# Summing five modulation vectors over the partitions with a GpSimd library instruction and an accumulating DMA instead of TensorE

## The chip, the cores and the metric

One core of a Trainium2 chip runs the whole kernel. The metric is the device time in microseconds (us) of one execution. The engines are named as in the profile: PE is TensorE (matmul), DVE is VectorE, ACT is ScalarE, POOL is GpSimd, and SP is SyncE, which here only issues DMAs.

## The reference

Two layers run over 256 latent tokens (x) and 256 context tokens (ctx) of width 1024. Each layer is a half-step SwiGLU, a token mixer (layer 0: neighbourhood attention, layer 1: a short gated convolution), and another half-step SwiGLU. Each sub-layer is modulated by vectors that come from a conditioning vector `c` through one large matrix `ada_w`:

```python
s_c = jax.nn.silu(c)
for i in range(DEPTH):                                   # DEPTH = 2
    m = (s_c @ ada_w[i] + ada_b[i]).reshape(B, N_MOD, 1, D)      # 9 vectors of 1024
    x = half_step_ffn(x, m[:, 0], m[:, 1], m[:, 2], ffn_w_in[i, 0], ffn_w_out[i, 0], ...)
    hx = modulate(x, m[:, 3], m[:, 4])                   # x * (1 + scale) + shift
    y_lat = attention or convolution of hx
    x = post_norm_update(x, y_lat, m[:, 5], 1.0, ...)    # LayerNorm(alpha*x + w*gate*y)
    x = half_step_ffn(x, m[:, 6], m[:, 7], m[:, 8], ffn_w_in[i, 1], ffn_w_out[i, 1], ...)
```

A vector is written (l, m): layer l, number m of nine. The change concerns the last five, (1,4) to (1,8).

## The kernel before

**The matmuls.** Every fp32 product of the layers is made of three fp32r matmuls: a weight block is loaded raw (`w1r`, `w2r`, by `wunit`), ACT copies its high part (`w1h`, line 210), DVE subtracts for the low part (`w1l`, line 213), and `mmu` (lines 164 to 167) multiplies high by high, high by low and low by high. PE's order is the program's own (a manual schedule); on DVE, ACT, POOL and SP a scheduler orders the instructions, and each engine then runs its list strictly in that order.

**A SwiGLU** (`ffn`) has 11 panels of `ffn_w_in`, each with four weight units and two token tiles, then a product with `ffn_w_out`. When a panel's PSUM bank is full, ACT makes `sil` (line 478) and DVE multiplies it with the other half of the bank (line 479). Four steps later PE transposes the two `sil` tiles (`gT`, line 487), ACT copies the result to `gh`, and DVE makes `gl` (line 113).

**The modulation vectors** are made in the background of these panels by `ada`. For one vector it loads eight 128 x 1024 blocks of `ada_w` (`ar`, line 303, on SP) and DVE accumulates each, times a per-partition scalar, into a tile `acc` of 128 x 1024 (lines 294 and 296, two halves of 512). When all vectors of a group are accumulated, and a few steps later, PE sums `acc` over the partitions by a matmul with ones (`ps`, tile name `ada`, line 327), DVE adds the bias row `adab` (line 328, tile `adar`), and SP writes the rows to `scr` in DRAM (line 330). From there `fold_cols` (tile `mrow`, line 360) and `mod_rows` (tile `gate`, line 345) read them back for the LayerNorm that uses them.

Behind attention there are three such groups: (1,4) and (1,5) during the second SwiGLU of layer 0, (1,6) and (1,7) during the first of layer 1, and (1,8) during the last. The pool `hp` is re-opened behind attention; `acc` has two buffers.

**POOL** does little there: two small instructions per LayerNorm tile (`rs`, lines 402 and 403), and a memset of `adab`.

Of the kernel before, what the change touches and what calls it, by code (L numbers as in the profile page):

```python
# [2 lines left out]

# [6 lines left out]
F32 = mybir.dt.float32  # L10
F32R = mybir.dt.float32r
AF = mybir.ActivationFunctionType
ALU = mybir.AluOpType
# [3 lines left out]
P = 128  # L17
D = 1024
FF = 2816
KC = D // P  # L20
# [50 lines left out]
def backbone_kernel(  # L71
# [6 lines left out]
    nc = tc.nc  # L78
    sync = nc.sync
# [8 lines left out]
    hp = phase.__enter__()  # L88
# [6 lines left out]
    def nm(s):  # L95
        uid[0] += 1
        return f"{s}_{uid[0]}"
# [10 lines left out]
    def tpb(s="tp"):  # L108
        return bank("tp", s)
# [125 lines left out]
    ones = cp.tile([P, 32], F32, tag="ones", name="ones")  # L235
    ident = cp.tile([P, P], F32, tag="ident", name="ident")
    make_identity(nc, ident)
    lnc = cp.tile([P, 2], F32, tag="lnc", name="lnc")
# [4 lines left out]
    warm = cp.tile([1, 1], F32, tag="warm", name="warm")  # L243
# [24 lines left out]
    scr = [tc.dram_tile([2, 9 * D], F32, name=f"scr{i}") for i in range(2)]  # L268
    xscr = tc.dram_tile([2 * P, D], F32, name="xscr")


    bias_rows = []
    gate_ins = []

    def ada(vecs):


        acc = {}

        def accumulate(l, m, k, w):  # L280
            with ExitStack() as st:
                for i in gate_ins:
                    st.enter_context(tc.issue_after(i.ins))
                for i, vec in enumerate(vecs):
                    if vec[:2] != (l, m):
                        continue
                    if k == 0:
                        a = hp.tile([P, D], F32, tag="acc", bufs=2, name=nm("acc"))
                        acc[i] = [a[:, 0:512], a[:, 512:D]]
                    sc = cst[:, k, vec[2]:vec[2] + 1]  # L290
                    for h in range(2):
                        src, a = w[:, h * 512:(h + 1) * 512], acc[i][h]
                        if k == 0:
                            nc.vector.tensor_scalar(a, src, sc, None, op0=ALU.mult)
                        else:
                            nc.vector.scalar_tensor_tensor(out=a, in0=src, scalar=sc, in1=a,  # L296
                                                           op0=ALU.mult, op1=ALU.add)

        loaded = []
        for l, m in dict.fromkeys((l, m) for l, m, _ in vecs):  # L300
            for k in range(KC):
                w = hp.tile([P, D], F32, tag="ar", bufs=3, name=nm("ar"))
                sync.dma_start(w, ada_w[l, k * P:(k + 1) * P, m * D:(m + 1) * D])
                loaded.append((l, m, k, w))
                if len(loaded) > (ADA_LAG if gate_ins else 0):
                    accumulate(*loaded.pop(0))
                yield 1
        while loaded:
            accumulate(*loaded.pop(0))
            if loaded:  # L310
                yield 1
        n = 2 * len(vecs)
        if not bias_rows:
            bias_rows.append(hp.tile([P, 512], F32, tag="adab", name=nm("adab")))
            nc.gpsimd.memset(bias_rows[0], 0.0)
        bt = bias_rows[0]
        for i, (l, m, v) in enumerate(vecs):
            sync.dma_start(bt[64 * i:64 * i + 64:32], ada_b[l, m * D:(m + 1) * D].rearrange("(a b) -> a b", b=512))
        yield 1
        yield 1  # L320
        yield 1
        rows = hp.tile([P, 512], F32, tag="adar", name=nm("adar"))
        ps = tpb("ada")
        for i in range(len(vecs)):
            for h in range(2):
                j = 2 * i + h
                nc.tensor.matmul(ps[32 * j:32 * j + 32, :], ones, acc[i][h], start=True, stop=True)  # L327
        nc.vector.tensor_tensor(out=rows[:32 * n], in0=ps[:32 * n], in1=bt[:32 * n], op=ALU.add)
        for i, (l, m, v) in enumerate(vecs):
            sync.dma_start(scr[l][v, m * D:(m + 1) * D].rearrange("(a b) -> a b", b=512),  # L330
                           rows[64 * i:64 * i + 64:32, :])
        yield 1
# [3 lines left out]
    def stream(*groups):  # L336
        for g in groups:
            yield from ada(g)
            made[0] += 1
            if made[0] == ADA_SLOW:  # L340
                background[1] = ADA_FAST
# [359 lines left out]
    for q, (k0, n) in enumerate(steps):  # L701
        nxt = start_step(*steps[q + 1]) if q < 4 else iter(())
        for g in range(6 * n):
            for _ in range(NS[min(q, 2)][g]):
                next(nxt, 0)
            k = k0 + g // 6
# [319 lines left out]
    hp = phase.__enter__()  # L1026
# [35 lines left out]
    for i in range(len(steps) + LAG + V_LAG):  # L1062
# [27 lines left out]
        j = i - LAG - V_LAG  # L1090
# [14 lines left out]
    hTs, later = box  # L1105
    phase = tc.tile_pool(name="ph2", bufs=1)
    hp = phase.__enter__()
    bias_rows.clear()
    ext[0] = 3

    set_background(stream([(1, 4, 0), (1, 5, 0)]), 0.35, HOLD)
# [16 lines left out]
    w = sc_w_in[0]  # L1128
# [103 lines left out]
```

## Time and profile before

| what | value |
| --- | --- |
| median of three runs | 1262.23 us (1261.55 to 1262.94) |
| span of the profiled execution | 1259.9 us |
| granted PE clock | 0.998 |
| busy: PE, DVE, ACT, POOL | 1245.4, 952.5, 589.9, 41.4 us |
| matmuls of line 327, all ten groups | 76 records, three groups (20 records) behind attention |

The profiled execution is known by its span, from the first to the last instruction; the profile gives no other time for it, and the median of the runs lies 2.3 us above that span. A row of the timeline has start, duration (of x instructions in a row), engine, line, operation, out<-in with shapes, and in brackets how long the engine idled before it and who released it. Matmul ends are modelled and successive matmuls overlap, so distances between starts tell what one costs. SPq is SP's queue, where only the issue of a DMA is seen.

### The profile page before, as it was taken

How to read it: one execution, taken by the hardware profiler on the slowest of the kernel's cores; microseconds unless marked ns; L12 is line 12 of the kernel's file. 1: busy time of each engine (PE TensorE's matmuls, PEld its weight loads, DVE VectorE, ACT ScalarE, POOL GpSimd, SP SyncE). 2: the span in 40 equal slices, each digit the busy share in tenths (PEclk: the TensorE clock that was granted, in tenths of full speed). 3: DMA queues.
4: the chain of work that ended last, by engine and by line, in shares of the span. 5: the costliest groups of instructions: out<-in, count | busy, mean ns of one | idle time of the engine just before them, and what ended most of it. 6: DMA issues, size and time to landing. Idle time of an engine off the chain costs nothing.

```text
span 1259.9 us, 17303 instructions
## 1 busy us (share of the span) xinstructions
PE 1245.4 (99%) x5922; PEld 1007.2 (80%) x5922; DVE 952.5 (76%) x1678; ACT 589.9 (47%) x1152; POOL 41.4 (3%) x71
## 2 busy tenths in 40 slices
PE   9999999999999999999999999999999999999997
PEld 6787778777878877877888788888788887888786
DVE  3699987888878877889898546988546788876546
ACT  2432132312326456687655435655435644655431
POOL 0000000000001011121000000000000000000000
PEclk9999999999999999999999999999999999999999
DMA  9976678878842744465899645898645764886641
GB/s 300 310 241 215 197 239 280 269 255 266 300 149 85 217 93 92 93 130 170 256 342 318 225 144 169 285 340 268 214 145 170 247 202 131 262 289 184 223 158 55
DMA packets 202776, 268.59 MB, mean 213 GB/s; under 512 B 30090, under 2 KB 149362, under 8 KB 202688
## 3 DMA queue, kind: packets, MB, share of 16 engines
q1 hardware_dynamic: 202652, 267.48, 67.3%
q8 instruction: 46, 0.75, 0.2%
q14 instruction: 42, 0.34, 0.1%
q10 hardware_dynamic: 36, 0.02, 0.0%
HBM read 265.27 MB, written 2.17 MB: 212 GB/s over the span
## 4 chain that ended last, share of the span: by engine, by line
PE 92%; DVE 3%; ACT 3%; issue 1%; DMA 0%; POOL 0%; DVEq 0%; SPq 0%; ACTq 0%; POOLq 0%
PE f L679 19%; PE w L164 17%; PE w L167 17%; PE w L165 17%; PE wkv L164 2%; PE wkv L165 2%; PE wkv L167 2%; PE wc L164 2%; PE wc L167 2%; PE wc L165 2%; PE gT L487 1%; PE ada L608 1%; PE ada L327 1%; PE S L971 1%; ACT pr L979 1%
## 5 line engine op out<-in xcount | busy, mean ns | idle before, releaser
L210 ACT ACTIVATE w1h<-w1r 128x512 fp32r<-128x512 f32 (+1 forms) x352 | 199.8, 620 | 180.4 <-DMA w1r<-in_ffn_w_in_dram 73.3
L213 DVE TENSOR_TENSOR w1l<-w1r,w1h 128x512 fp32r<-128x512 f32 (+1 forms) x352 | 222.9, 679 | 44.6 <-ACT w1h L210 43.3
L164 PE MATMUL w<-w1h,hTh 128*128 128x512 f32 x528 | 209.4, 397 | 0.9 <-ACT hTh L112 0.9
L165 PE MATMUL w<-w1l,hTh 128*128 128x512 f32 x528 | 206.0, 390 | 0.2 <-DVE w1l L213 0.2
L296 DVE SCALAR_TENSOR_TENSOR acc<-ar,cst,acc 128x512 f32<-128x512 f32 x266 | 186.0, 746 | 15.4 <-DMA ar<-in_ada_w_dram 15.4
L164 PE MATMUL w<-w2h,gh 128*128 128x512 f32 (+1 forms) x446 | 173.4, 389 | 0.0
L165 PE MATMUL w<-w2l,gh 128*128 128x512 f32 (+1 forms) x446 | 172.1, 386 | 0.0
L213 DVE TENSOR_TENSOR w2l<-w2r,w2h 128x512 fp32r<-128x512 f32 x176 | 114.3, 688 | 76.0 <-ACT w2h L210 75.2
L210 ACT ACTIVATE w2h<-w2r 128x512 fp32r<-128x512 f32 x176 | 101.6, 624 | 146.0 <-PE w L167 103.6
L167 PE MATMUL w<-w1h,hTl 128*128 128x512 f32 x528 | 163.2, 390 | 0.3 <-DVE hTl L113 0.2
L167 PE MATMUL w<-w2h,gl 128*128 128x512 f32 (+1 forms) x446 | 136.1, 386 | 0.0
L679 PE MATMUL f<-h0h,w1h 128*128 128x512 f32 x352 | 133.3, 394 | 0.4 <-DVE h0h L634 0.4
L679 PE MATMUL f<-h0l,w1h 128*128 128x512 f32 x352 | 133.2, 391 | 0.0
L679 PE MATMUL f<-h0h,w1l 128*128 128x512 f32 x352 | 132.7, 390 | 0.0
L164 PEld LDWEIGHTS w<-w1h,hTh 128*128 128x128 f32 x528 | 99.2, 188 | 23.8 <-ACT hTh L112 1.7
L167 PEld LDWEIGHTS w<-w1h,hTl 128*128 128x128 f32 x528 | 98.9, 188 | 22.4 <-DVE hTl L113 1.5
L165 PEld LDWEIGHTS w<-w1l,hTh 128*128 128x128 f32 x528 | 99.2, 188 | 20.2 <-DVE w1l L213 0.6
L164 PEld LDWEIGHTS w<-w2h,gh 128*128 128x128 f32 x446 | 83.8, 188 | 19.2 <-issue 1.7
L165 PEld LDWEIGHTS w<-w2l,gh 128*128 128x128 f32 x446 | 83.8, 188 | 16.6
L167 PEld LDWEIGHTS w<-w2h,gl 128*128 128x128 f32 x446 | 83.3, 188 | 17.1
L679 PEld LDWEIGHTS f<-h0h,w1h 128*128 128x128 f32 x352 | 65.9, 189 | 18.8 <-issue 4.2
L679 PEld LDWEIGHTS f<-h0l,w1h 128*128 128x128 f32 x352 | 65.6, 188 | 14.3 <-issue 0.6
(186 smaller groups left out, 1684.5 us busy)
## 6 DMA issues: line engine op xcount, KB each, us to landing
w1r<-in_ffn_w_in_dram SPq DMA_DIRECT2D x340, 256.0 KB
ar<-in_ada_w_dram SPq DMA_DIRECT2D x128, 512.0 KB
w2r<-in_ffn_w_out_dram SPq DMA_DIRECT2D x88, 512.0 KB
ar<-in_ada_w_dram SPq DMA_DIRECT2D x32, 256.0 KB
wkvr<-in_na_w_qkv_dram SPq DMA_DIRECT2D x32, 256.0 KB
wcr<-in_sc_w_in_dram SPq DMA_DIRECT2D x32, 256.0 KB
wqr<-in_na_w_qkv_dram SPq DMA_DIRECT2D x8, 512.0 KB
wor<-in_na_w_out_dram SPq DMA_DIRECT2D x8, 512.0 KB
```

Of the source, the lines that this page charges most:

```text
L164: nc.tensor.matmul(ps, lh, rh, start=first and i == 0, stop=False)
L165: nc.tensor.matmul(ps, lh, rl, start=False, stop=False)
L167: nc.tensor.matmul(ps, ll, rh, start=False, stop=last and i == n - 1)
L210: nc.scalar.activation(hi[:, a:a + m // W_HI], raw[:, a:a + m // W_HI], AF.Copy)
L213: nc.vector.tensor_tensor(out=lo[:, a:b], in0=raw[:, a:b], in1=hi[:, a:b].bitcast(F32), op=ALU.subtract)
L296: nc.vector.scalar_tensor_tensor(out=a, in0=src, scalar=sc, in1=a, op0=ALU.mult, op1=ALU.add)
L327: nc.tensor.matmul(ps[32 * j:32 * j + 32, :], ones, acc[i][h], start=True, stop=True)
L487: nc.tensor.transpose(ps[:, j * 256 + i * P:j * 256 + (i + 1) * P], g[:, j * P:(j + 1) * P], ident)
L608: nc.tensor.matmul(ps[o:o + 32, 0:m], cst[:, a * kt + i, :], w[:, i, j, :], start=(a == 0 and i < 2), stop=(a == last and i >= kt - 2))
L679: nc.tensor.matmul(ps, w, hT0[k][part == 1], start=(k == part == 0), stop=(k == KC - 1 and part == 1))
L971: nc.tensor.matmul(banks[i], (qh, qh, ql)[f][ps, qs], (kh, kl, kh)[f][ps, :], start=f == 0, stop=f == 2)
L979: nc.scalar.activation(pr, S, AF.Exp, bias=mx[:, 0:1], accum_out=mx[:, 1:2])
```

## The change

From the end of attention on (`on_pool`), a vector is no longer summed on PE. As soon as its last block is accumulated, `summed` gives its `acc` to a library instruction of POOL, `partition_all_reduce`, which writes the sum over the partitions to all 128 partitions of a tile `red` (one buffer), and POOL issues a DMA that adds the first partition of `red` to `scr` in DRAM. For this the bias `ada_b` of the five vectors is copied into `scr` beforehand, in one DMA on SP. Behind a group's last vector, POOL reads `red` once in a one-element add (`warm`).

```diff
+from concourse.bass_isa import ReduceOp
...
+    on_pool = [False]
...
-                        a = hp.tile([P, D], F32, tag="acc", bufs=2, name=nm("acc"))
-                        acc[i] = [a[:, 0:512], a[:, 512:D]]
+                        acc[i] = hp.tile([P, D], F32, tag="acc", bufs=2, name=nm("acc"))
...
+            if on_pool[0] and k == KC - 1:
+                for i, vec in enumerate(vecs):
+                    if vec[:2] == (l, m):
+                        summed(i)
+
+        def summed(i):
+            l, m, v = vecs[i]
+            red = hp.tile([P, D], F32, tag="red", name=nm("red"))
+            nc.gpsimd.partition_all_reduce(red, acc[i], P, ReduceOp.add)
+            nc.gpsimd.dma_start(scr[l][v:v + 1, m * D:(m + 1) * D], red[0:1], accum_op=ALU.add)
+            if i == len(vecs) - 1:
+                nc.gpsimd.tensor_tensor(out=warm, in0=red[0:1, 0:1], in1=lnc[0:1, 0:1], op=ALU.add)
...
+        if on_pool[0]:
+            yield 1
+            return
         n = 2 * len(vecs)
...
-                nc.tensor.matmul(ps[32 * j:32 * j + 32, :], ones, acc[i][h], start=True, stop=True)
+                nc.tensor.matmul(ps[32 * j:32 * j + 32, :], ones, acc[i][:, h * 512:(h + 1) * 512], start=True, stop=True)
...
-    bias_rows.clear()
+    on_pool[0] = True
+    sync.dma_start(scr[1][0, 4 * D:9 * D].rearrange("(a b) -> a b", a=16), ada_b[1, 4 * D:9 * D].rearrange("(a b) -> a b", a=16))
```

How the instructions stand now (the line numbers of the changed kernel are up to 16 higher). POOL's list behind attention, before: two `rs` instructions for each LayerNorm tile, and the memset of the bias rows.

```order
L402 TENSOR_TENSOR rs_5661<-mv_5659,lnc 128x1
L403 TENSOR_TENSOR rs_5661<-rs_5661,lnc 128x1
L315 MEMSET adab_6712 128x512
L402 TENSOR_TENSOR rs_5744<-mv_5742,lnc 128x1
L403 TENSOR_TENSOR rs_5744<-rs_5744,lnc 128x1
L402 TENSOR_TENSOR rs_7409<-mv_7407,lnc 128x1
L403 TENSOR_TENSOR rs_7409<-rs_7409,lnc 128x1
```

The same place of POOL's list now. A bare ISA row is a change of the instruction library; `red<-acc` is the library's sum, which waits for DVE's last accumulation.

```order
L418 TENSOR_TENSOR rs_5744<-mv_5742,lnc 128x1
L419 TENSOR_TENSOR rs_5744<-rs_5744,lnc 128x1
L307 ISA
L307 ISA red_6385<-acc_6101 128x1024
L308 DMA scr_117<-red_6385 16x1x64
L307 ISA red_6716<-acc_6433 128x1024
L308 DMA scr_117<-red_6716 16x1x64
L310 ISA
L310 TENSOR_TENSOR warm<-red_6716,lnc 1x1
L418 TENSOR_TENSOR rs_7404<-mv_7402,lnc 128x1
```

The first library change has nothing to wait for and follows attention's last `rs`; the sums, their DMAs, the change back and `warm` now stand ahead of the next LayerNorm's `rs`.

PE's list in the second SwiGLU of layer 0, before: four matmuls with `ones` between two weight units.

```order
L164 MATMUL w_1269_6765<-w1h_6803,hTh_5819 128x512
L165 MATMUL w_1269_6765<-w1l_6804,hTh_5819 128x512
L167 MATMUL w_1269_6765<-w1h_6803,hTl_5820 128x512 x2
L327 MATMUL ada_6824<-acc_6100,ones 32x512 x2
L327 MATMUL ada_6824<-acc_6429,ones 32x512 x2
L164 MATMUL w_1268_6758<-w1h_6833,hTh_5724 128x512
L165 MATMUL w_1268_6758<-w1l_6834,hTh_5724 128x512
```

PE's list there now.

```order
L165 MATMUL w_1270_6769<-w1h_6807,hTh_5820 128x512
L166 MATMUL w_1270_6769<-w1l_6808,hTh_5820 128x512
L168 MATMUL w_1270_6769<-w1h_6807,hTl_5821 128x512 x2
L165 MATMUL w_1269_6762<-w1h_6828,hTh_5724 128x512
L166 MATMUL w_1269_6762<-w1l_6829,hTh_5724 128x512
```

Only the matmuls with `ones` are gone, here and in the two later groups (ten in all); DVE's list has lost three `adar` rows and is otherwise the same, with the panels' `w1l`, `sil` and `gl` in the same places between the accumulations.

SP's list in the same SwiGLU, before, at the place to which a read of `scr` moves (`mrow` is the 8 x 128 read of (1,4) for a later LayerNorm; it stood 27 rows further on, behind ten loads of `w2r`).

```order
L205 DMA w1r_6722<-in_ffn_w_in_dram 128x2x256 x2
L205 DMA w1r_6749<-in_ffn_w_in_dram 128x2x256 x2
L205 DMA w1r_6772<-in_ffn_w_in_dram 128x2x256 x2
L205 DMA w1r_6802<-in_ffn_w_in_dram 128x2x256 x2
L303 DMA ar_6597<-in_ada_w_dram 128x1024
```

SP's list there now.

```order
L206 DMA w1r_6726<-in_ffn_w_in_dram 128x2x256 x2
L206 DMA w1r_6753<-in_ffn_w_in_dram 128x2x256 x2
L206 DMA w1r_6776<-in_ffn_w_in_dram 128x2x256 x2
L376 DMA mrow_8707<-scr_117 8x128
L206 DMA w1r_6806<-in_ffn_w_in_dram 128x2x256 x2
L316 DMA ar_6601<-in_ada_w_dram 128x1024
```

The read of (1,4) now stands among the weight loads and waits there for POOL's DMA. The reads of (1,6) and (1,7) move forward in the same way in the next SwiGLU: (1,6) to just ahead of two `ar` loads, (1,7) to behind the second load of `w2r`. The ten small SP DMAs of the old way (bias in, rows out) are gone, and the one copy of the bias stands early in the first SwiGLU of layer 0.

More of the change, by code (lines that the diff above doesn't have):

```diff
@@ L287, in accumulate @@
                     if k == 0:
-                        a = hp.tile([P, D], F32, tag="acc", bufs=2, name=nm("acc"))
-                        acc[i] = [a[:, 0:512], a[:, 512:D]]
+                        acc[i] = hp.tile([P, D], F32, tag="acc", bufs=2, name=nm("acc"))
                     sc = cst[:, k, vec[2]:vec[2] + 1]
                     for h in range(2):
-                        src, a = w[:, h * 512:(h + 1) * 512], acc[i][h]
+                        src, a = (c[:, h * 512:(h + 1) * 512] for c in (w, acc[i]))
                         if k == 0:
```

## The prediction

> **What bounds the kernel now.** The page's first part comes first, then the busy times of the stage that the change touches, then the timeline there.
>
> ```profile
> PE 1245.4 (99%) x5922; PEld 1007.2 (80%) x5922; DVE 952.5 (76%) x1678; ACT 589.9 (47%) x1152; POOL 41.4 (3%) x71
> ...
> 597.00:784.00 187.00, 187.00 (x857) 153.45 (x856) 135.85 (x231) 96.59 (x185) 1.63 (x3) 1.00 0.74 246
> ```
>
> The second row is the second SwiGLU of layer 0 (length; then PE, PE's weight loads, DVE, ACT and POOL busy). PE has no gap in 187 us, so what is taken from PE shortens the stage, and what makes PE wait lengthens it. DVE is busy for 73% and POOL is free.
>
> **What is removed.** Busy time of the `ada` matmuls in three windows of 20 us (PE, weight loads, DVE), and PE's timeline without and with them:
>
> ```profile
> 700.00:720.00 20.00, 1.06 (x8) 0.16 (x8) 0.68 (x1) 1.00 0.60 205
> 880.00:900.00 20.00, 1.06 (x8) 0.16 (x8) 0.68 (x1) 1.00 0.67 225
> 1170.00:1190.00 20.00, 1.05 (x4) 0.14 (x4) 0.68 (x1) 1.00 0.58 191
> ```
>
> ```profile
> 698.00 0.61 PE L167 MATMUL w<-w1h,hTl 128*128 128x512 f32 x2
> ...
> 698.68 0.39 PE L165 MATMUL w<-w1l,hTh 128*128 128x512 f32 x1
> ...
> 703.94 0.61 PE L167 MATMUL w<-w1h,hTl 128*128 128x512 f32 x2
> 704.48 1.06 PE L327 MATMUL ada<-acc,ones 128*32 128x512 f32 x8
> ...
> 705.81 0.39 PE L165 MATMUL w<-w1l,hTh 128*128 128x512 f32 x1
> ```
>
> From an L167 pair to the second matmul behind it PE takes 698.68 - 698.00 = 0.68 us; with a group of four `ada` matmuls between them 705.81 - 703.94 = 1.87 us. A group costs 1.19 us and not the sum of its matmuls' times, since its four 32-column matmuls run beside each other; the group of two takes as long (1.05 against 1.06). Three groups: 3 x 1.19 = 3.6 us off PE, on the path. The three `adar` adds (0.68 us each) leave DVE, which PE did not wait for: nothing. The ten small DMAs that leave SP, and the one copy that comes, lie among loads issued far ahead of use (below): nothing.
>
> **What is added: how long a library sum takes.** No row shows one. The nearest is POOL's two-input add:
>
> ```profile
> L883 POOL TENSOR_TENSOR bias<-bias,wmask 128x256 f32<-128x256 f32 x28 | 22.4, 801 | 128.1 <-DMA bias<-in_na_rpb_dram 119.7 <-DVE pT L113 6.7 <-DVE mx L977 1.6
> ```
>
> At 0.80 us for 256 columns one pass over 1024 columns is 3.2 us. Lower end: one pass, 3.2 us. Upper end: eight groups of 16 partitions taken one after the other, 8 x 3.2 = 25.6 us. I take two and a half passes, 8 us: one to combine the groups, one to hand the result back to all 128 partitions, half a pass for adding within a group. That lies nearer the add's row, since the groups can work side by side. Call this time X. POOL itself has room for five of them (1.63 us busy in 187). The changes of library are unseen too, between nothing and a few passes; the first of each group stands directly behind the `rs` of the sub-layer before, long ahead of the sum, and the second between the sums and the next `rs`, where POOL is idle. I take nothing for both.
>
> **What X does to DVE.** POOL and DVE have met before, in attention:
>
> ```profile
> 413.90 0.79 POOL L883 TENSOR_TENSOR bias<-bias,wmask 128x256 f32<-128x256 f32 x1 [10.34 <-DMA bias<-in_na_rpb_dram]
> ```
>
> ```profile
> 412.80 2.44 DVE L213 TENSOR_TENSOR wkvl<-wkvr,wkvh 128x512 fp32r<-128x512 f32 x3
> ...
> 690.79 1.89 DVE L213 TENSOR_TENSOR w1l<-w1r,w1h 128x512 fp32r<-128x512 f32 x3
> ```
>
> Three subtractions of the same shape take 1.89 us alone and 2.44 us with POOL's add among them: DVE lost 0.55 of the add's 0.79 us. If that holds for a library sum, DVE stands still for X at its next instruction with two SBUF inputs, five times. By the row's share, 0.55/0.79 or 70%, it would lose 5.6 us each, and the whole change would come to about nothing (below). I count all of X: the missing 0.24 us is an edge, DVE finishing the instruction under way while POOL's already counts, and a longer instruction has that edge once.
>
> The Trainium skill says so outright (SBUF — State Buffer, "Who interferes with whom"): the read port is an exclusive lock for the whole instruction, against a DVE instruction with two SBUF inputs too. The row agrees for an ordinary add; no run here shows it for a library instruction. By the page alone the sum is the 1273.5 us below, by the row's share about 1262.5 us.
>
> **From DVE to PE.** DVE runs in order, so the panel's second `sil` (L479) waits behind the blocked `w1l`, and PE's transposes `gT` wait for it. A sum can start where its accumulation (L296) ends; behind each end I list where DVE idled up to the next second `sil` (the second sum's end lies just ahead of the 690.79 row above):
>
> ```profile
> 656.68 0.74 DVE L296 SCALAR_TENSOR_TENSOR acc<-ar,cst,acc 128x512 f32<-128x512 f32 x1
> ...
> 662.27 0.42 DVE L479 TENSOR_TENSOR sil<-sil,w 128x256 f32<-128x256 f32 x1 [0.84 <-ACT sil L478]
> ...
> 693.88 1.29 DVE L213 TENSOR_TENSOR w1l<-w1r,w1h 128x512 fp32r<-128x512 f32 x2 [1.21 <-ACT w1h L210]
> ...
> 696.35 0.42 DVE L479 TENSOR_TENSOR sil<-sil,w 128x256 f32<-128x256 f32 x1 [0.85 <-ACT sil L478]
> ...
> 830.05 2.73 DVE L296 SCALAR_TENSOR_TENSOR acc<-ar,cst,acc 128x512 f32<-128x512 f32 x4
> ...
> 838.26 1.29 DVE L213 TENSOR_TENSOR w1l<-w1r,w1h 128x512 fp32r<-128x512 f32 x2 [1.27 <-ACT w1h L210]
> 839.47 0.85 DVE L479 TENSOR_TENSOR sil<-sil,w 128x256 f32<-128x256 f32 x2
> ...
> 874.34 2.73 DVE L296 SCALAR_TENSOR_TENSOR acc<-ar,cst,acc 128x512 f32<-128x512 f32 x4
> ...
> 882.88 1.29 DVE L213 TENSOR_TENSOR w1l<-w1r,w1h 128x512 fp32r<-128x512 f32 x2 [1.43 <-ACT w1h L210]
> ...
> 885.35 0.42 DVE L479 TENSOR_TENSOR sil<-sil,w 128x256 f32<-128x256 f32 x1 [0.85 <-ACT sil L478]
> ...
> 1146.20 1.41 DVE L296 SCALAR_TENSOR_TENSOR acc<-ar,cst,acc 128x512 f32<-128x512 f32 x2
> ...
> 1150.60 0.69 DVE L113 TENSOR_TENSOR gl<-gT,gh 128x512 fp32r<-128x512 f32 x1 [0.47 <-ACT gh L112]
> 1152.02 1.29 DVE L213 TENSOR_TENSOR w1l<-w1r,w1h 128x512 fp32r<-128x512 f32 x2 [0.73 <-ACT w1h L210]
> 1154.76 1.29 DVE L213 TENSOR_TENSOR w1l<-w1r,w1h 128x512 fp32r<-128x512 f32 x2 [1.45 <-ACT w1h L210]
> ...
> 1157.23 0.42 DVE L479 TENSOR_TENSOR sil<-sil,w 128x256 f32<-128x256 f32 x1 [0.84 <-ACT sil L478]
> ```
>
> The transposes that use these five `sil` pairs:
>
> ```profile
> 665.74 0.60 PE L487 MATMUL gT<-ident,sil 128*128 128x128 f32 x4
> ...
> 699.82 0.60 PE L487 MATMUL gT<-ident,sil 128*128 128x128 f32 x4
> ...
> 843.37 0.60 PE L487 MATMUL gT<-ident,sil 128*128 128x128 f32 x4
> ...
> 888.82 0.60 PE L487 MATMUL gT<-ident,sil 128*128 128x128 f32 x4
> ...
> 1160.70 0.60 PE L487 MATMUL gT<-ident,sil 128*128 128x128 f32 x4
> ```
>
> Each `sil` ends 3.05 us ahead of its `gT` (665.74 - 662.69, 699.82 - 696.77, 843.37 - 840.32, 888.82 - 885.77, 1160.70 - 1157.65). DVE can lose this and its idle time on the way before PE feels it: 3.05 + 0.84 = 3.9; + 1.21 + 0.85 = 5.1; + 1.27 = 4.3; + 1.43 + 0.85 = 5.3; + 0.47 + 0.73 + 1.45 + 0.84 = 6.5 us, 25.1 us in all. PE waits X less these: 5 x 8 - 25.1 = 14.9 us.
>
> **What else waits.** SP's moved reads of `scr` now wait for POOL's DMA, with weight loads behind them. The slots, and how far ahead weights are loaded:
>
> ```profile
> 666.04 7.31 SPq L205 DMA_DIRECT2D w1r<-in_ffn_w_in_dram  x8
> ...
> 841.14 1.66 SPq L303 DMA_DIRECT2D ar<-in_ada_w_dram  x2
> ...
> 880.14 15.80 SPq L205 DMA_DIRECT2D w2r<-in_ffn_w_out_dram  x7
> ```
>
> ```profile
> L210 ACT ACTIVATE w2h<-w2r x44: 614/623/634, 698.7 to 766.2; 128x512 fp32r<-128x512 f32 x44
> ...
> L205 SPq DMA_DIRECT2D w2r<-in_ffn_w_out_dram x22: 367/368/390, 691.5 to 756.8; - x22
> ```
>
> ```profile
> L164 PE MATMUL w<-w2h,gh x88: 389/389/508, 719.7 to 780.5; 128*128 128x512 f32 x88
> ```
>
> The slots lie near 671.5 (behind three of four load pairs), 841 and 884.7 (behind two of seven). With X = 8 the sums end near 666, 841.4 and 885.7 (accumulation's end, 0.6 us for the DVE instruction under way, X). A 512 KB load is used 7.2 us after its issue (698.7 - 691.5), so the 4 KB write needs less, and SP waits up to 2, 8 and 8 us. PE uses the first `w2` unit 28.2 us after its issue, 20 us later than needed: SP's waits are covered while they stay under that, and I cost them at nothing. The read of (1,8), `gate`, stands behind the last panel's loads and nine of `w2r`, long behind its sum. If this cover went, the `ar` loads would be late next, and with them DVE's accumulations.
>
> **Sum.** -3.6 + 14.9 = +11.3 us on a profiled span of 1259.9 us. The median of the runs stands 2.3 us above the span and has the same stages, so the difference goes onto it: 1262.2 + 11.3 = 1273.5 us.
>
> **Rivals.** *Hidden (ends on the other side).* The library sum reads in small pieces between which DVE gets in, or X is under 4 us: then no place loses more than it has, and only PE's 3.6 us remain, 1258.6 us. For it: DVE idles 27% of the stage, and a sum spends time between cores rather than on SBUF. Against it: the attention row, where POOL held DVE for most of its instruction. The point that decides is a standstill of 5.5 us: 1.6 + 0.4 + 1.2 + 0.2 = 3.4, about the 3.6 gained.
> *Long sum.* The cores take turns, X = 25.6: 5 x 25.6 - 25.1 - 3.6 = +99 us, 1361 us, and SP's waits pass 20 us as well. The Trainium skill (GPSIMD Engine Reference, section 3.2) gives 247.7 us for a partition-axis `tensor_reduce` of 128 x 2048; half of it, an estimate of 124 us, would make the kernel several hundred us slower. It is another instruction, and no run here shows either.
> *No effect.* The matmuls' place is taken by another PE wait of the same size, 1262 us. Against it: no wait in that stage is there to surface.
>
> **How the numbers follow.** DVE blocked with X from 6 to 12 us: 0.55, time 1264 to 1293.5 (5 x 12 - 25.1 - 3.6 = +31.3), likeliest 1273.5. Hidden: 0.31, 1258 to 1261. Blocked for 5 to 6 us, or no effect: 0.08, within 2.5 us of 1262. Long sum or slow library changes: 0.06. A measurement tells about 0.2%, or 2.5 us, from no change. Faster 0.28 (hidden, less a little), same 0.09, slower 0.63. The range goes from the hidden case, 1258, to X = 10.5, or +23.8, at 1286; the rest of the blocked case and the long sum lie above.
>
> **What would show it.** Right: `ada` rows behind attention gone; POOL rows of about 8 us on `red`; beside each a DVE `w1l` or `acc` instruction of about X instead of 0.7 us; and PE waits of 1.5 to 4 us at L487 <- DVE sil L479, smallest at the last sum. Wrong: `w1l` keeps its 0.7 us beside `red`; or PE stays gapless though DVE is held, so that the slack was larger; or PE waits for `w1l` and not for `sil`, so that loads were late.

## The result and the profile after

| what | before | after |
| --- | --- | --- |
| median of nine runs each | 1262.13 us (1261.55 to 1262.94) | 1258.44 us (1258.20 to 1260.24) |
| ratio | | 0.9975, 95% interval 0.9965 to 0.9984 |
| span of the profiled execution | 1259.9 us | 1256.7 us |
| granted PE clock | 0.998 | 0.998 |

The kernel became 3.7 us faster; 11.3 us slower was forecast. The time is that of the rival *Hidden*. In after, `w1l` is L214, `sil` L495, `gT` L503, `rs` L418, the sum L307.

The page's busy times of after:

```profile
PE 1241.4 (99%) x5902; PEld 1006.9 (80%) x5902; DVE 966.5 (77%) x1675; ACT 590.2 (47%) x1152; POOL 85.0 (7%) x83
```

PE has 20 matmul records less and is 4.0 us less busy. POOL is 43.6 us busier, and DVE 14.0 us busier although it has three instructions less: DVE was held, and PE did not notice. The sums, in POOL's timeline (start, duration, and in brackets the idle time before):

```profile
657.24 8.14 POOL L307 PARTITION_ALL_REDUCE red<-acc  x1 [59.79 <-DVE acc L297]
...
688.43 7.68 POOL L307 PARTITION_ALL_REDUCE red<-acc  x1 [21.62 <-DVE acc L297]
...
707.99 0.18 POOL L310 TENSOR_TENSOR warm<-red,lnc 1x1 f32<-1x1 f32 x1 [10.78 <-issue]
...
832.74 7.66 POOL L307 PARTITION_ALL_REDUCE red<-acc  x1 [47.81 <-DVE acc L297]
...
876.11 7.68 POOL L307 PARTITION_ALL_REDUCE red<-acc  x1 [34.41 <-DVE acc L297]
...
1145.55 6.46 POOL L307 PARTITION_ALL_REDUCE red<-acc  x1 [78.86 <-DVE acc L297]
```

A sum takes 6.5 to 8.1 us. In DVE's timeline, in windows narrow enough to show one instruction by itself, one `w1l` beside each sum is long:

```profile
659.66 4.67 DVE L214 TENSOR_TENSOR w1l<-w1r,w1h 128x512 fp32r<-128x512 f32 x1 [0.28 <-ACT w1h L211]
...
690.05 0.69 DVE L114 TENSOR_TENSOR gl<-gT,gh 128x512 fp32r<-128x512 f32 x1
690.65 4.43 DVE L214 TENSOR_TENSOR w1l<-w1r,w1h 128x512 fp32r<-128x512 f32 x1
...
834.93 4.42 DVE L214 TENSOR_TENSOR w1l<-w1r,w1h 128x512 fp32r<-128x512 f32 x1
...
878.33 4.42 DVE L214 TENSOR_TENSOR w1l<-w1r,w1h 128x512 fp32r<-128x512 f32 x1
...
1145.93 5.03 DVE L214 TENSOR_TENSOR w1l<-w1r,w1h 128x512 fp32r<-128x512 f32 x1
```

Such an instruction takes 0.69 us otherwise, so DVE lost 3.98, 3.74, 3.73, 3.73 and 4.34 us. Two things are to be read from the rows together. The held instruction starts 2.4, 2.2, 2.2, 2.2 and 0.4 us behind the sum's start. And it ends about 1.05 us ahead of the sum's end (690.65 + 4.43 = 695.08 against 688.43 + 7.68 = 696.11), having needed 0.69 us itself: DVE is free again some 1.7 us before the sum ends. The hold is one block, but shorter than the instruction.

PE's two longest waits in after (us in total, times, longest):

```profile
PE f L255 <- POOL ident masks.py:199: 2.2, 1, 2.2
PE w L165 <- ACT hTh L113: 1.3, 2, 0.7
```

No wait of `gT` on `sil` is among PE's waits, long or short. Where the gain appears, by POOL's `rs` at the ends of the SwiGLUs, before:

```profile
775.90 0.53 POOL L402 TENSOR_TENSOR rs<-mv,lnc 128x1 f32<-128x1 f32 x1 [178.30 <-DVE mv L400]
...
964.90 0.52 POOL L402 TENSOR_TENSOR rs<-mv,lnc 128x1 f32<-128x1 f32 x1 [178.70 <-DVE mv L400]
...
1060.07 0.19 POOL L402 TENSOR_TENSOR rs<-mv,lnc 128x1 f32<-128x1 f32 x1 [84.86 <-DVE mv L400]
...
1246.72 0.19 POOL L402 TENSOR_TENSOR rs<-mv,lnc 128x1 f32<-128x1 f32 x1 [177.84 <-DVE mv L400]
```

And after:

```profile
774.57 0.53 POOL L418 TENSOR_TENSOR rs<-mv,lnc 128x1 f32<-128x1 f32 x1 [66.40 <-DVE mv L416]
...
962.65 0.53 POOL L418 TENSOR_TENSOR rs<-mv,lnc 128x1 f32<-128x1 f32 x1 [69.35 <-DVE mv L416]
...
1057.88 0.19 POOL L418 TENSOR_TENSOR rs<-mv,lnc 128x1 f32<-128x1 f32 x1 [84.86 <-DVE mv L416]
...
1243.34 0.19 POOL L418 TENSOR_TENSOR rs<-mv,lnc 128x1 f32<-128x1 f32 x1 [81.41 <-DVE mv L416]
```

After is ahead by 1.3 us behind the first group, 2.3 behind the second, 2.2 behind the convolution, which has none, and 3.4 behind the third: one step of about 1.2 us for each group of matmuls removed.

SP's waits on the new DMA (the moved reads of `scr`):

```profile
SPq L376 <- DMA scr<-red: 5.6, 2, 3.4
```

### The profile page after: what moved, and what is told of

Its sections match the earlier page's. It is cut to its first block, busy times and chain, and to the rows that moved or that the text cites. A ratio compares the mean times of both kernels' runs of the same rounds, so it can differ in the third digit from the quotient of the medians.

```text
span 1256.7 us, 17284 instructions
## 1 busy us (share of the span) xinstructions
PE 1241.4 (99%) x5902; PEld 1006.9 (80%) x5902; DVE 966.5 (77%) x1675; ACT 590.2 (47%) x1152; POOL 85.0 (7%) x83
## 4 chain that ended last, share of the span: by engine, by line
PE 92%; ACT 3%; DVE 3%; issue 1%; DMA 1%; POOL 0%; DVEq 0%; SPq 0%; POOLq 0%; ACTq 0%
PE f L695 19%; PE w L165 17%; PE w L168 17%; PE w L166 17%; PE wkv L165 2%; PE wkv L166 2%; PE wkv L168 2%; PE wc L165 2%; PE wc L168 2%; PE wc L166 2%; PE gT L503 1%; PE ada L624 1%; PE hT L437 1%; PE S L987 1%; PE wo L165 1%
## 5 line engine op out<-in xcount | busy, mean ns | idle before, releaser
L214 DVE TENSOR_TENSOR w1l<-w1r,w1h 128x512 fp32r<-128x512 f32 (+1 forms) x352 | 241.7, 734 | 35.5 <-ACT w1h L211 33.2
L214 DVE TENSOR_TENSOR w2l<-w2r,w2h 128x512 fp32r<-128x512 f32 x176 | 114.1, 688 | 72.0 <-ACT w2h L211 71.2
```

The lines of the kernel that those rows point to most:

```text
L214: nc.vector.tensor_tensor(out=lo[:, a:b], in0=raw[:, a:b], in1=hi[:, a:b].bitcast(F32), op=ALU.subtract)
```

## The experiments

The theory after the result, T: the whole gain is the matmuls' time; a sum costs DVE about 4 us of its 7.7, and the slack of its place covers that. The rivals were that the sums cost something and hide a larger gain (C), that the gain comes from the other edits, the moved DMAs above all (R), that a sum never matters to PE through DVE (N), and that DVE is held for a whole instruction, with something else shortening it here (Q). The expectations below name rivals run by run: what is C here is R in the first of them, and N is S in the third.

**The sums left out.** POOL's DMA adds the first partition of `acc` unsummed; the sum over the partitions is not computed, and the one-element add `warm` is left out with it.

```diff
-            red = hp.tile([P, D], F32, tag="red", name=nm("red"))
-            nc.gpsimd.partition_all_reduce(red, acc[i], P, ReduceOp.add)
-            nc.gpsimd.dma_start(scr[l][v:v + 1, m * D:(m + 1) * D], red[0:1], accum_op=ALU.add)
...
+            nc.gpsimd.dma_start(scr[l][v:v + 1, m * D:(m + 1) * D], acc[i][0:1], accum_op=ALU.add)
```

> The changed kernel without the library sums: POOL's DMA adds the first partition of acc itself, so the sum over the partitions is left out. Theory T (the sums hold DVE for about 4 us each and this fits into DVE's slack; the whole gain is the three groups of matmuls that left PE): the sums cost PE nothing, so 1258.4 us as in the changed kernel, within 1 us. Rival R (the sums do cost PE some us and something else gained more than 3.6 us): clearly faster than the changed kernel, 1256 us or less.

Measured: 1258.40 us (1257.47 to 1259.85), ratio to before 0.9974 (0.9965 to 0.9984); the changed kernel's is 0.9975. Without the sums no `w1l` is long (minimum, median, maximum in ns):

```profile
L214 DVE TENSOR_TENSOR w1l<-w1r,w1h x352: 550/683/695, 12.9 to 1168.9; 128x512 fp32r<-128x512 f32 x168, 128x384 fp32r<-128x384 f32 x8
```

So five holds of DVE cost nothing that can be measured. C falls.

**The matmuls put back beside the sums.** PE again multiplies by ones behind each group; the result is not used.

```diff
         if on_pool[0]:
+            yield 1
+            yield 1
+            yield 1
+            ps = tpb("ada")
+            for i in range(len(vecs)):
+                for h in range(2):
+                    j = 2 * i + h
+                    nc.tensor.matmul(ps[32 * j:32 * j + 32, :], ones, acc[i][:, h * 512:(h + 1) * 512], start=True, stop=True)
```

> The changed kernel with the ten matmuls with ones back on PE at their old distance behind the accumulation, their result unused; library sums and accumulating DMAs stay. Theory T: three groups of 1.19 us, 1258.4 + 3.6 = 1262.0 us, the same as before the change. Rival R (the gain came from elsewhere, such as the small DMAs that left SP or the adds that left DVE): stays near 1258.4 us.

Measured: 1262.01 us (1261.03 to 1262.57), ratio to before 1.0003 (0.9994 to 1.0012). The ten matmuls cost 1262.01 - 1258.44 = 3.6 us, which is the whole gain. R falls.

**A sum of twice the width.** Each sum reads `acc` twice, as 2048 columns, into a bf16 tile; the second half is not used, and the result is rounded to bf16. The order on all other engines is unchanged.

```diff
-            red = hp.tile([P, D], F32, tag="red", name=nm("red"))
-            nc.gpsimd.partition_all_reduce(red, acc[i], P, ReduceOp.add)
...
+            red = hp.tile([P, 2, D], mybir.dt.bfloat16, tag="red", name=nm("red"))
+            nc.gpsimd.partition_all_reduce(red, acc[i].unsqueeze(1).to_broadcast([P, 2, D]), P, ReduceOp.add)
...
```

> The changed kernel with each library sum taken over acc twice in one instruction (2048 columns, the second half unused, result rounded to bf16); the order of PE, DVE, ACT and SP is unchanged. Theory T: one hold of DVE of about 8.5 us instead of 4.3 us, a loss of about 8 us at each sum, and PE waits what exceeds the slacks of 3.9, 5.1, 4.3, 5.3 and 6.5 us: 5 x 8 - 25.1 = 15 us, about 1273 us, with the waits at the gT transposes on sil. Rival S (the slack between sil and gT is not what hides the sums; DVE runs tens of us ahead of PE everywhere): no more than 1 us, 1258 to 1260 us. SP will wait some 4, 11 and 11 us for the three reads of scr, and late ar loads could add a few us under either.

Measured: 1279.15 us (1277.90 to 1279.86), ratio 1.0137 (1.0123 to 1.0151). In DVE's timeline at the first sum, six `w1l` take 12.62 us instead of 3.69 (5 x 0.60 + 0.69), a loss of 8.9 us, and at the second, five take 11.41 us instead of 3.09, a loss of 8.3 us; PE's longest waits beside it:

```profile
657.16 12.62 DVE L214 TENSOR_TENSOR w1l<-w1r,w1h 128x512 fp32r<-128x512 f32 x6
...
697.00 11.41 DVE L214 TENSOR_TENSOR w1l<-w1r,w1h 128x512 fp32r<-128x512 f32 x5
```

```profile
PE gT L503 <- DVE sil L495: 14.6, 5, 4.3
```

PE now waits just where the prediction had put the waits, five times, 14.6 us in all: 4.3, 2.6, 4.0, 2.2 and 1.5 us. The same reading at the other three places gives losses of 8.3, 8.3 and 8.9 us. A loss less its wait is the slack: 4.6, 5.7, 4.3, 6.1 and 7.4 us, where the prediction had 3.9, 5.1, 4.3, 5.3 and 6.5. So each slack was right to 0.9 us, and never larger in the prediction than it is. That the expectation (8 us each, 15 us of waits) came out so closely is in part luck, since loss and slack are both about half a microsecond larger. N falls.

The kernel is 20.7 us slower than the changed one, though, and the waits are 14.6. The rest is the clock. PE's busy time and granted clock (fourth column) around the first wait and behind the fourth, of 2.2 us:

```profile
660.00:670.00 10.00, 5.88 (x26) 1.00 0.42 146
670.00:675.00 5.00, 4.83 (x16) 0.66 0.72 203
675.00:680.00 5.00, 5.00 (x24) 1.00 1.02 328
...
905.00:910.00 5.00, 2.79 (x14) 1.00 0.66 211
910.00:915.00 5.00, 5.00 (x24) 1.00 0.60 205
```

Behind a gap of 4.3 us PE is granted 0.66 of its clock for about 5 us. Behind the second and third wait (2.6 and 4.0 us) it is 0.86 and 0.80, and 0.54 and 0.78, in two such slices each; behind the fourth and the fifth (2.2 and 1.5 us) it stays at 1.00. Over the stretch with the first four waits (length; PE, weight loads, DVE, ACT, POOL busy; clock), first this kernel, then the changed one:

```profile
640.00:965.00 325.00, 311.68 (x1386) 255.17 (x1386) 251.18 (x372) 152.11 (x289) 60.50 (x14) 0.98 0.69 227
```

```profile
640.00:965.00 325.00, 324.77 (x1474) 267.13 (x1473) 244.60 (x393) 160.38 (x302) 38.55 (x16) 1.00 0.72 238
```

0.02 x 325 = 6.5 us (in slices of 5 us, five are below 1.00, and what they lack times 5 us adds up to 6.8), and 14.6 + 6.5 = 21.1 against the 20.7 measured. On average over the five, a wait of PE costs about 1.4 times its length here; the surcharge comes with the three longer ones.

**How long the hold is, by itself.** A kernel without the layers: eight sums beside chosen work of DVE on 512 columns.

```diff
+    def two(o):
+        nc.vector.tensor_tensor(out=o, in0=xa[:, 0:512], in1=xb[:, 0:512], op=ALU.subtract)
+    def one(o):
+        nc.vector.tensor_tensor(out=o, in0=bank, in1=xb[:, 0:512], op=ALU.subtract)      # bank is in PSUM
...
+    segment("A", D, 0, [])
+    segment("B", D, 3, [two] * 16)
+    segment("C", D, 3, [two] * 3 + [one] + [two] * 12)
+    segment("E", D, 3, [one] * 16)
+    segment("F", D, 3, [scale] * 24)
+    segment("G", 512, 3, [two] * 16)
+    segment("H", 512, 0, [])
+    segment("I", D, 0, [])
```

> None of the layers; eight library sums, one after the other, beside chosen DVE work. A: alone, 1024 columns. B: beside sixteen subtractions with two SBUF inputs. C: the same with one instruction that reads PSUM and SBUF as the fourth. E: beside sixteen instructions with one SBUF and one PSUM input. F: beside twenty-four tensor-scalar instructions on SBUF. G: like B with 512 columns. H: 512 columns alone. I: 1024 alone again. Theory P (the sum holds the second read port only while it reads, about 4.35 us for 1024 columns, and works on for 1.7 us without it): in B one DVE instruction is about 4 us longer, in E none is, in G about 2 us; A and I last 6 to 6.5 us, and C and B differ only in when the hold begins. Rival Q (the port is held for the whole instruction and the hold in the kernel began late for another reason): in B DVE loses 6 us or more.

Measured, in POOL's timeline: A alone, B beside subtractions of two SBUF inputs, E beside subtractions with one input in PSUM, H alone on 512 columns:

```profile
7.12 6.11 POOL L110 PARTITION_ALL_REDUCE redA<-accA  x1 [6.69 <-DVE accA L109]
...
17.36 6.48 POOL L110 PARTITION_ALL_REDUCE redB<-accB  x1 [4.13 <-DVE accB L109]
...
57.01 6.11 POOL L110 PARTITION_ALL_REDUCE redE<-accE  x1 [13.34 <-DVE accE L109]
...
107.26 3.23 POOL L110 PARTITION_ALL_REDUCE redH<-accH  x1 [11.21 <-DVE accH L109]
```

And DVE's sixteen instructions beside B, E and G (the last a sum of 512 columns):

```profile
17.18 15.79 DVE L96 TENSOR_TENSOR sink<-xa,xb 128x512 f32<-128x512 f32 x16
...
56.83 11.56 DVE L99 TENSOR_TENSOR sink<-bank,xb 128x512 f32<-128x512 f32 x16
...
92.27 13.50 DVE L96 TENSOR_TENSOR sink<-xa,xb 128x512 f32<-128x512 f32 x16
```

Beside E nothing is lost: an input in PSUM keeps DVE out of the conflict for the whole sum. Beside B DVE loses 15.79 - 11.56 = 4.2 us to a sum of 6.48, beside G 1.9 us to one of 3.60. For these subtractions the hold is some 55 to 65% of the sum and grows with its width. Q, the whole instruction, falls for them.

F is held as well, though its tensor-scalar instructions have only one SBUF input. Two of the 24 are long, beside a sum that runs from 72.59 to 78.80:

```profile
72.87 4.64 DVE L102 TENSOR_SCALAR sink<-xa 128x512 f32<-128x512 f32 x1
...
77.55 1.54 DVE L102 TENSOR_SCALAR sink<-xa 128x512 f32<-128x512 f32 x1
79.12 0.43 DVE L102 TENSOR_SCALAR sink<-xa 128x512 f32<-128x512 f32 x1
```

Such an instruction takes 0.43 us otherwise, so F loses 4.21 + 1.11 = 5.3 us of a sum of 6.21, more than B, and part of it at the sum's end, where B is already free. Having one SBUF input is no protection by itself.

**The sum made twice.** Is it the longest single hold that counts, or what DVE loses ahead of one `sil`?

```diff
             nc.gpsimd.partition_all_reduce(red, acc[i], P, ReduceOp.add)
+            nc.gpsimd.partition_all_reduce(red, acc[i], P, ReduceOp.add)
```

> The changed kernel, with each sum made twice in a row into the same tile. DVE is held twice for about 4.2 us with some 2 us free between. Theory T (what counts is how much DVE loses ahead of one `sil`, against a slack of 3.9 to 6.5 us): the second hold falls behind the next `sil`, or only partly ahead of it, so PE waits 0 to 4 us in all, 1258 to 1263 us. Rival S (the two holds add up as in the sum of 2048 columns): PE waits of about 14 us, 1275 to 1280 us.

Measured: 1277.35 us (1276.75 to 1279.10), ratio 1.0120 (1.0106 to 1.0134). The expectation of T missed, and rival S (1275 to 1280 us) had it. DVE's timeline at the first sum, and PE's longest wait:

```profile
656.11 12.37 DVE L214 TENSOR_TENSOR w1l<-w1r,w1h 128x512 fp32r<-128x512 f32 x6
668.41 0.74 DVE L496 TENSOR_TENSOR sil<-sil,w 128x256 f32<-128x256 f32 x2
```

```profile
PE gT L504 <- DVE sil L496: 12.9, 5, 4.2
```

Six `w1l` stand between the sum's start and the second `sil`, and between the two holds DVE gets through only three of them (from 661.66 to 663.54), so both holds fall ahead of the same `sil`: a loss of 8.7 us against a slack of 3.9, a wait of 4.2 us there and 12.9 in all. The rule of the theory stands, its application was wrong: losses ahead of one `sil` add up, whether or not DVE runs between them. With 12.9 us of waits and again a clock of 0.98 over the same 325 us (6.5 us) this makes 19.4; measured against the changed kernel: 18.9.

**More groups on POOL.** If a sum is free, the seven groups ahead of attention are the obvious next step. The first kernel moves the groups from the fourth on, the second all but the first (the bias is copied ahead of them, and the groups left on PE put bias and rows into the tile `red`, for space).

```diff
         for g in groups:
+            on_pool[0] = made[0] >= 3          # the second kernel: >= 1
             yield from ada(g)
...
+    for l, v, m0, m1 in ((0, 0, 5, 9), (1, 0, 0, 4)):      # the second: from (0, 3) on
+        sync.dma_start(scr[l][v, m0 * D:m1 * D].rearrange("(a b) -> a b", a=16), ...)
```

> The groups from the fourth on, (0,5) to (1,3), are summed on POOL as well: here the two vectors of a group are complete some 70 us apart and share no wait for `acc`. Four groups of `ones` matmuls leave PE. Theory T: 4 x 1.19 = 4.8 us less, 1253.7 us, no PE wait on `sil`, and eight more DVE rows of 4 to 5 us, each beside a row of POOL. Rival D (DVE's total work decides): 8 x 4 = 32 us more on DVE, slower than the 1258.4 us.

> All groups but the first are summed on POOL, so six more groups of `ones` matmuls leave PE. Theory T (a sum holds DVE for about 4.4 us, which the slack of a panel covers, and all the gain is the matmuls' time): 6 x 1.19 = 7.1 us more, 1251.3 us, if DVE's slack in the first SwiGLU is as large as behind attention and `acc` comes free in time. Against it: in the second and third group both vectors are complete together, so the second sum starts about 9 us behind the first, and the first accumulation of the next group must wait for it on DVE; where that wait passes the slack, PE waits for `sil` or for `w1l`, and the gain is smaller or gone. Rival D (the time follows DVE's total work, which the sums make longer by 12 x 4 = 48 us): slower than 1258 by 10 us or more.

Measured: 1288.49 us (1288.21 to 1290.78), ratio 1.0206 (1.0192 to 1.0220), for four groups; 1304.69 us (1302.82 to 1305.76), ratio 1.0333 (1.0318 to 1.0347), for six. Both expectations of T missed by far. PE's waits with four groups, from 180 to 385 us, where the eight new sums lie:

```profile
PE f L695 <- DVE w1l L214: 13.1, 4, 4.9
PE w L166 <- DVE w2l L214: 8.9, 3, 4.2
```

The same stretch (length; PE, weight loads, DVE, ACT, POOL busy; clock) with four groups moved and, in the second fence, in the changed kernel:

```profile
180.00:385.00 205.00, 182.13 (x755) 146.40 (x754) 177.91 (x226) 49.63 (x87) 58.73 (x20) 0.94 0.72 236
```

```profile
180.00:385.00 205.00, 205.00 (x917) 165.73 (x916) 165.62 (x269) 58.87 (x103) 0.00 (x0) 1.00 0.77 251
```

The sums last 6.1 to 6.5 us here, and the two of a group start 22 to 26 us apart, not the 70 expected; the slack is another. In the first SwiGLU PE does not wait for `sil` but for the weights' low parts `w1l` and `w2l` themselves, seven times, 22.0 us for eight sums. Together with the clock, 0.06 x 205 = 12.3 us, and less four groups of matmuls, 4.8 us, that is 29.5; measured against the changed kernel: 30.1.

The instruction that is held is another, too. At six of the eight sums it is the first accumulation of the next vector (L295), a tensor-scalar instruction with one SBUF input besides its column of scalars, as in F. Two of them in the changed kernel, and beside the first sum here:

```profile
665.52 0.87 DVE L295 TENSOR_SCALAR acc<-ar,cst 128x512 f32<-128x512 f32 x2
```

```profile
192.92 5.16 DVE L295 TENSOR_SCALAR acc<-ar,cst 128x512 f32<-128x512 f32 x2
```

In this stretch 14 of them take 35.0 us, in the changed kernel 6.2. With the `w2l` and the `gl` that are held at the two other sums (4.3 and 3.2 us), DVE loses some 36 us, and 22.0 us of waits reach PE. So only some 14 us are covered, 1.8 us a sum, where the prediction counted 25.1 us for the five places behind attention.

The rival that the time follows DVE's total work gave 32 us for four groups and 48 us for six, and 30 and 46 us were measured. It comes near by chance: the 14 us that are covered are about what the clock adds, and the rival says nothing of the five sums behind attention that cost nothing. With six groups there is in addition a direct wait of DVE, the one expected against T:

```profile
DVE acc L295 <- POOL red L307: 13.6, 2, 7.5
```

The first accumulation of the next group waits for `acc`, since two vectors are complete together and share one `red`. Why so little is covered ahead of attention, place by place, was not measured; that DVE is only 81% busy there in the changed kernel (165.62 of 205) did not help.

**When the hold begins.** The second small kernel (again no layers) lets DVE run at its dense pitch of 0.60 us, with changing output tiles.

```diff
+        nc.vector.tensor_tensor(out=outs[count[0] % 4], in0=xa[:, h:h + 512], in1=xb[:, h:h + 512], op=ALU.subtract)
...
+    segment("B", D, 3, [two] * 20)
+    segment("C", D, 3, [two] * 3 + [one] + [two] * 16)
```

> No layers are computed: six sums of 128 x 1024 beside chosen DVE work of 512 columns with changing output tiles, so that DVE runs at its dense pitch of about 0.60 us. What is open is why the hold begins 1.6 to 2.1 us behind the sum's start at the first four places of the changed kernel and 0.4 us at the last. Rival 1 (a dense row of instructions with two SBUF inputs keeps POOL out until DVE has a gap or an instruction with a PSUM input): in B and J the hold begins late or only behind the last of the 20, and in C and L about when the instruction with the PSUM input runs. Rival 2 (it is something of the sum itself): the hold begins 0.2 to 0.7 us behind the sum's start in every segment, as in the first small kernel.

Beside B the second subtraction is held (18.55, 0.43 us behind the sum's start at 18.12); beside C, whose first three instructions are the same, none of them is, but the one behind the instruction with the PSUM input, 2.23 us behind the sum's start at 38.05:

```profile
17.95 0.68 DVE L101 TENSOR_TENSOR o<-xa,xb 128x512 fp32r<-128x512 f32 x1
...
18.55 5.02 DVE L101 TENSOR_TENSOR o<-xa,xb 128x512 fp32r<-128x512 f32 x1
...
39.68 0.68 DVE L104 TENSOR_TENSOR sink<-bank,xb 128x512 f32<-128x512 f32 x1
40.28 4.42 DVE L101 TENSOR_TENSOR o<-xa,xb 128x512 fp32r<-128x512 f32 x1
```

Both kinds of start of the changed kernel are there again, with durations of 5.02 and 4.42 us against 5.03 and 4.42 there. The other segments take sides with neither rival. J (accumulations) is held 0.49 us behind the sum's start; K and L, subtractions and accumulations mixed, 1.04 us behind it, in L well ahead of the instruction with the PSUM input; and in the first small kernel, whose C has the same order, the hold falls ahead of that instruction. So rival 1 fails in B, J and L, rival 2 in C, K and L, and what decides stays open.

## Why the prediction was wrong

- **What is removed** was right. 1.19 us a group, 3.6 us in all; the matmuls put back cost 3.6 us, and each of the three SwiGLUs that lost a group adds about 1.2 us to the lead over before.
- **How long a sum takes** came out near: X was put at 8 us, and the sums take 7.7 us at the median. This is in part luck: alone a sum takes 6.11 us, no run shows the two and a half passes, and the rest is its wait for DVE, which the prediction did not have.
- **"I count all of X" is the step that failed.** DVE lost 3.7 to 4.3 us, 49 to 67% of the sum. The 0.24 us that were missing in attention's row (0.55 lost of 0.79) I called an edge that a longer instruction has once. Scaling the row's share, the 70% that the prediction names and sets aside, would have been nearer, with 5.6 us each; even that was too much. A sum has parts in which it doesn't exclude such a subtraction, 1.7 us at its end here, and waits up to about 2 us at its start before it holds DVE. PE stayed gapless though DVE was held, a sign that the prediction names, but because the hold was shorter and not because the slack was larger.
- The Trainium skill (SBUF — State Buffer, "Who interferes with whom") gives the read port for the whole instruction. The rows differ: 4.2 us lost beside a library sum of 6.48 us. The other half of the section, that a DVE instruction with at most one SBUF input, outside the 2-port performance modes, doesn't contend, agrees where the other input is in PSUM: nothing lost in sixteen instructions beside a sum of 6.11 us. The tensor-scalar instructions with one SBUF input were held (5.3 us beside a sum of 6.21); whether they ran in such a mode no run here shows. By the first half I weighed the wrong ending as the likelier.
- **The slacks, 25.1 us,** were right to 0.9 us each, and on the small side: with DVE's loss about doubled they came out at 4.6, 5.7, 4.3, 6.1 and 7.4 us. In the changed kernel the losses of 3.98, 3.74, 3.73, 3.73 and 4.34 us are all covered. The first is 0.1 us above the 3.9 of the prediction and under the 4.6 measured; its second `sil` ends at 665.60, just as its transposes start. A loss within its place's slack costs nothing, and the forecast turned on that.
- **The price of a wait** was sized too small, though it did not come into play. I counted a PE wait at its length; with the clock that is granted behind them, 14.6 us of waits cost 21. Had all of X been held, the kernel would by this ratio have been some 6 us slower still than forecast, an estimate.
- **What else waits** was right: SP waits 5.6 us in two pieces, inside the 20 us of cover. The library changes were left unpriced; idle time put down to "issue", 8.3 to 10.8 us, stands ahead of `warm`, and nothing waits for POOL then.
- The rival *Hidden* gave 1258.6 us and had the right time for partly the wrong reason: DVE doesn't get in between small pieces, it is held in one block, only a shorter one.

## What to carry to other kernels

A conflict between two engines is paid only in what it adds beyond the slack between the blocked engine and the one that bounds the kernel, so work out that slack at every place, add up all holds that fall ahead of one use, and price the hold by its own length, not by the duration of the instruction that causes it. That length depends on the instruction that is blocked. Five of these sums were free behind attention, and eight cost 30 us ahead of it, where another tile was the late one. Where a wait of some microseconds does reach TensorE, add to its length the slower clock behind it.

## What was not expected of the hardware

- `partition_all_reduce` over 128 partitions takes 6.11 us for 1024 columns and 3.23 us for 512 with nothing beside it, and 6.5 to 8.1 us beside DVE's work in the changed kernel: a busy DVE makes the sum up to 2 us longer.
- The sum excludes DVE subtractions with two SBUF inputs for about 4.2 us (1024 columns) or 1.9 us (512 columns), tensor-scalar instructions with one SBUF input for 5.3 us (1024 columns), and subtractions with one input in PSUM not at all.
- Behind a PE gap of 4.3 us the granted clock was 0.66 over 5 us; behind gaps of 2.2 and 1.5 us in the same kernel it stayed at 1.00.
